# Two MLPs with thirteen Strassen-Winograd units and residual sums in place, and a ReLU bias in the state-space mixer

## The chip, the cores and the metric

The kernel runs on one core of a Trainium2 chip. The metric is the device time of one execution in microseconds (us), lower is better. The core has a matrix engine (TensorE, PE in the profile, with its weight loads as PEld), VectorE (DVE), ScalarE (ACT), GpSimd (POOL) and SyncE (SP), which issues nearly all transfers. Each engine works through its own queue in order and waits on semaphores for the others.

## The reference

A trunk of two layers works on 512 tokens and 16 learned ones ahead of them, 528 columns of 1024 features, in float32. Layer 0 mixes with retention and gated delta-rule heads, layer 1 with a Mamba-2 state-space mixer; each mixer is followed by an MLP with squared ReLU, and each of the four sublayers ends in a layer norm:

```python
h = layer_norm(DN_ALPHA * h + mix, ln1_w[i], ln1_b[i])
h = layer_norm(DN_ALPHA * h + sq_relu_mlp(h, mlp_w1[i], mlp_w2[i]), ln2_w[i], ln2_b[i])

def sq_relu_mlp(h, w1, w2):                      # w1: 1024 x 4096, w2: 4096 x 1024
    return jnp.square(jax.nn.relu(h @ w1)) @ w2
```

In the state-space mixer the attention of a chunk is weighted by `exp(gcum_t - gcum_s)` for s up to t, where `gcum` is the running sum of the log decays of a head.

## The kernel before

**Layout and precision.** Activations lie transposed, features on the 128 partitions in 8 tiles and the tokens along the columns, in two halves of 272 and 256 columns (256 and 256 from the second residual of layer 1 on, where the learned tokens are dropped). Every product of float32 numbers is done as three matmuls of reduced-precision parts (L172 to L174): the activation is kept as a pair `hi`, `lo`, with `hi` the rounded value and `lo` the rest, and each weight tile is fetched and then split on the chip (`split`, L152 on ScalarE and L153 on VectorE). A weight tile of 1024 columns is one such split. `phase` runs over output tiles and evacuates each half from PSUM through a function it is given; in layer 1's MLP a third entry of the activation list holds both halves side by side, so that one matmul covers 512 columns.

**Order.** The program is written as straight code with generators beside it: `spawn` adds one to a list, and `tick` advances each by one step, so that a task's instructions fall between the matmuls of the main line. A planner then places each engine's instructions, near to the order in which they are written, and gives out the buffers. Tiles of a kind (`m`: 24, `s`: 40, `w`: 12 for weights, `row`: 3) share a pool, and PSUM has 3 + 5 banks (`pm`, `px`).

**Layer norm.** `residual` sums `DN_ALPHA * h` and the product of a sublayer in `m` tiles r[half][tile]; `norm_after` transposes these, takes the statistics (L272), normalizes, transposes back (L330) and writes the next activation: `hi` by ScalarE (L337), the full value into a fresh `m` tile t by VectorE (L339), and `lo` as their difference by GpSimd, every fourth by VectorE (L340).

**The MLP.** The 4096 hidden features are 8 groups of 4 tiles. First products of a group (`w1`) give squared ReLUs by ScalarE, GpSimd (L435) and VectorE (L442); second products (`w2`) give a share of the sums over the hidden features for all 8 output tiles, each added to r by `evac0`. The first share finds no r yet: it takes `DN_ALPHA * hi + o` (L366) and then adds `DN_ALPHA * lo` (L367); later shares are one addition (L362). Groups 0 and 1 are done directly, groups 2 to 7 by `Unit`s: a unit does two hidden tiles by Strassen and Winograd's scheme, seven products of half the depth and half the columns (L500, 84 matmuls) in place of eight. It needs combinations of the weights, which `Unit.prepare` makes (L473 to L477 and five splits), and four combinations of the activation for each of 4 pairs of feature tiles, which `combos` makes once for an MLP from the `hi` and `lo` parts (L385 to L401) and splits again. `Four` does the second product of a group for 4 output tiles, with its weights fetched and split ahead. What comes first, up to the first unit's end, is called the head below:

```python
phase([([w1[l, f]], f) for f in range(GF)], hx, ev, ns, head=3, ready=ready)   # group 0
spawn(combos(pairs, nh, get))
for f in range(GF):                                                             # group 1, one tile
    phase([([w1[l, GF + f]], f)], hx, evn, ns)
    if f == 2:
        spawn(stages[0].gen)
    second(0, u, 2 * f, 2 * f + 2)                                              # and two of group 0's second
```

After the head, units and `Four`s alternate: unit (2,0), four (1,0), unit (2,1), four (1,1), up to group 7, whose second product is a `phase` that fetches its weights tile by tile (512 columns) and keeps back the last three output tiles: their half 0 is done for all three, then their half 1 (`tail=3`).

**The mixer's decays.** For each of 4 groups of 8 heads and 4 chunks of 128 columns, `loads` broadcasts `gcum` of the 8 heads over the partitions by a transfer into a `row` tile (128 x 1024). `decays` makes of it `exp(-relu(gcum_s - gcum_t))`: a subtraction on GpSimd (L1181), a ReLU and an exponential on ScalarE (L1182, L1183). GpSimd then multiplies by the chunk's products (L1197), and TensorE takes the result (L1241), together with an operand that VectorE writes (L1202). Beside this the convolutions of the next group of heads run (ScalarE L601 and L604, VectorE L603 and L606).

Of the kernel before, what the change touches and what calls it, by code (L numbers as in the profile page):

```python
# [57 lines left out]
def trunk(ctx: ExitStack, tc: tile.TileContext, a, out):  # L58
# [250 lines left out]
    def norm_after(r, ns, wcol, bcol):  # L309
# [5 lines left out]
        def task(hf):  # L315
# [11 lines left out]
            for m in range(KT):  # L327
# [10 lines left out]
                t = tl("m", n)  # L338
# [33 lines left out]
    def combos(pairs, nh, get):  # L372


        q = slice(0, nh), slice(nh, 2 * nh)

        def part(k, c, lo):
            return pairs[k][lo][:, q[c]].bitcast(F32)

        def diff(out, a, b, engine):  # L380
            engine.tensor_tensor(out, a, b, op=SUB)

        for k in range(4):
            d1, d3, e = tl("m", nh), tl("m", nh), tl("m", nh)
            G.tensor_tensor(d1, part(k, 1, 0), part(k, 0, 0), op=SUB)  # L385
            V.tensor_tensor(e, part(k, 1, 1), part(k, 0, 1), op=SUB)
            V.tensor_tensor(d1, d1, e, op=ADD)
            get(0, k, d1)
            yield
            G.tensor_tensor(d3, part(k + 4, 1, 0), part(k, 1, 0), op=SUB)  # L390
            V.tensor_tensor(e, part(k + 4, 1, 1), part(k, 1, 1), op=SUB)
            V.tensor_tensor(d3, d3, e, op=ADD)
            get(2, k, d3)
            yield
            d2, d4 = tl("m", nh), tl("m", nh)
            G.tensor_tensor(d2, part(k + 4, 1, 0), d1, op=SUB)
            V.tensor_tensor(d2, d2, part(k + 4, 1, 1), op=ADD)
            get(1, k, d2)
            yield
            G.tensor_tensor(d4, part(k + 4, 0, 0), d2, op=SUB)  # L400
            V.tensor_tensor(d4, d4, part(k + 4, 0, 1), op=ADD)  # L401
            get(3, k, d4)
            yield

    def mlp(l, hx, ns, ready, r, evac0, pairs):
# [41 lines left out]

        def second(c, u, m0, m1, tail=0):
            phase([([lambda m=m: wload(second_src(c, m), 512)], m) for m in range(m0, m1)], u,
                  lambda m, hf, o: evac0(m, hf, o, last=c == NG - 1), ns, tail=tail)  # L450
# [110 lines left out]
        u, ev = group()  # L561
        phase([([w1[l, f]], f) for f in range(GF)], hx, ev, ns, head=3, ready=ready)
        spawn(combos(pairs, nh, get))
        stages = []
        un, evn = group()
        groups = [(u, ev), (un, evn)] + [group() for _ in range(2, NG)]
        for c in range(2, NG):
# [947 lines left out]
```

## Time and profile before

| | |
|---|---|
| median of 3 executions | 1738.64 us (1734.0 to 1739.5) |
| the profiled execution | 1738.46 us, span 1736.7 us |
| mean granted TensorE clock | 0.982 |
| transfers | 158.05 MB, 91 GB/s on average |

A row of a group of instructions reads: line, engine, operation, output<-input by the program's names, shape, count, then busy time and the mean of one in ns, then the engine's idle time ahead of them and what ended it. A row in order of time begins with its start and length in us. A wait reads: who waited, for whom, us in total, times, the longest. A stretch reads: its bounds, its length, then the busy time and number of instructions of each engine, the granted TensorE clock, the share of the transfer engines and GB/s. A matmul's row lasts longer than the distance to the next, since they are pipelined; distances are taken from start to start.

### The profile page before, as it was taken

What the parts mean: (1) busy time and instruction counts of PE and PEld (TensorE: products, weight loads), DVE (VectorE), ACT (ScalarE), POOL (GpSimd) and SP (SyncE); (2) the same over time, 40 slices, a digit from 0 to 9 for tenths busy, and PEclk for the clock granted to TensorE, in tenths of its full rate; (3) what the DMA queues carried; (4) which work ended last, traced back from release to release, by engine and by line L of the source; (5) the groups of instructions that cost most, each with busy time, mean ns of one, the idle gap of its engine ahead of it and who ended that gap; (6) DMA issues with size and microseconds to landing.
All of it is one profiled execution on the core that took longest, in us unless ns stands there. A gap on an engine that the chain in (4) does not pass through costs nothing.

```text
span 1736.7 us, 30064 instructions
## 1 busy us (share of the span) xinstructions
PE 1674.2 (96%) x11896; PEld 1542.2 (89%) x11896; DVE 1199.8 (69%) x2383; ACT 700.9 (40%) x1354; POOL 351.1 (20%) x412
## 2 busy tenths in 40 slices
PE   9998999999999899999999998999999998999997
PEld 7897998899999889999998987888778987888886
DVE  5896666766437877767747876767564688777765
ACT  4432235554214344444424643545432434444431
POOL 1211210010003411111102145344410342111112
PEclk9998999999999999999999999999999999999999
DMA  7223212112222232222221443333223123222321
GB/s 243 82 91 86 88 47 84 46 54 84 87 74 68 73 104 98 98 98 98 79 71 62 137 121 92 102 112 98 91 67 110 55 91 110 98 98 98 101 73 69
DMA packets 93002, 158.05 MB, mean 91 GB/s; under 512 B 14077, under 2 KB 47229, under 8 KB 92605
## 3 DMA queue, kind: packets, MB, share of 16 engines
q1 hardware_dynamic: 92716, 155.87, 27.9%
q8 instruction: 93, 1.52, 0.4%
q14 instruction: 49, 0.39, 0.1%
q10 hardware_dynamic: 144, 0.26, 0.0%
HBM read 149.95 MB, written 6.15 MB: 90 GB/s over the span
## 4 chain that ended last, share of the span: by engine, by line
PE 79%; DVE 10%; DMA 4%; POOL 3%; ACT 2%; issue 2%; SPq 0%; POOLq 0%; DVEq 0%; ACTq 0%
PE pmm L172 18%; PE pmm L174 18%; PE pmm L173 18%; PE pmx L500 10%; PE pmm L500 4%; DVE w L153 2%; DVE s L603 2%; DMA row<-rd 1%; DMA w<-in_w 1%; PE pmx L1241 1%; PE pmx L270 1%; DMA du<-row 1%; POOL n L147 1%; PE pmx L1245 1%; ACT w L152 1%
## 5 line engine op out<-in xcount | busy, mean ns | idle before, releaser
L172 PE MATMUL pmm<-hh,w 128*128 128x256 f32 (+5 forms) x1528 | 472.9, 310 | 5.6 <-DVE m L366 2.8
L174 PE MATMUL pmm<-hh,w 128*128 128x256 f32 (+5 forms) x1528 | 459.4, 301 | 2.1 <-DVE w L153 2.1
L173 PE MATMUL pmm<-hl,w 128*128 128x256 f32 (+5 forms) x1528 | 458.4, 300 | 0.7 <-POOL hl L340 0.3
L153 DVE TENSOR_TENSOR w<-w,w 128x1024 fp32r<-128x1024 f32 (+2 forms) x269 | 323.7, 1205 | 142.0 <-PE pmm L173 67.6
L152 ACT CAST w<-w 128x1024 fp32r<-128x1024 f32 (+2 forms) x269 | 263.7, 981 | 373.7 <-PE pmm L174 137.1
L172 PE MATMUL pmm<-s,w 128*128 128x256 f32 (+2 forms) x1180 | 376.8, 319 | 4.3 <-DVE m L366 2.7
L174 PE MATMUL pmm<-s,w 128*128 128x256 f32 (+2 forms) x1180 | 375.5, 318 | 0.2 <-DVE w L153 0.2
L173 PE MATMUL pmm<-s,w 128*128 128x256 f32 (+2 forms) x1180 | 375.5, 318 | 0.0
L172 PEld LDWEIGHTS pmm<-hh,w 128*128 128x128 f32 (+2 forms) x1528 | 289.1, 189 | 20.9 <-issue 4.0
L173 PEld LDWEIGHTS pmm<-hl,w 128*128 128x128 f32 (+2 forms) x1528 | 289.0, 189 | 13.5 <-issue 2.4
L174 PEld LDWEIGHTS pmm<-hh,w 128*128 128x128 f32 (+2 forms) x1528 | 289.0, 189 | 11.4 <-DVE w L153 2.9
L172 PEld LDWEIGHTS pmm<-s,w 128*128 128x128 f32 x1180 | 222.3, 188 | 20.1 <-DVE m L366 3.2
L174 PEld LDWEIGHTS pmm<-s,w 128*128 128x128 f32 x1180 | 222.2, 188 | 15.8 <-DVE w L153 0.6
L173 PEld LDWEIGHTS pmm<-s,w 128*128 128x128 f32 x1180 | 222.2, 188 | 15.2 <-DVE s L1320 0.3
L435 POOL TENSOR_TENSOR m<-m 128x256 f32<-128x256 f32 (+2 forms) x128 | 89.0, 697 | 511.7 <-ACT m L433 499.4
L362 DVE TENSOR_TENSOR m<-m,pmm 128x256 f32<-128x256 f32 (+1 forms) x236 | 93.6, 416 | 71.7 <-PE pmm L174 71.5
L147 POOL TENSOR_TENSOR n<-n,neg 128x1 f32<-128x1 f32 (+2 forms) x58 | 39.8, 690 | 450.4 <-DVE n L146 426.4
L603 DVE SCALAR_TENSOR_TENSOR s<-s,pp,s 128x528 f32<-128x528 f32 x120 | 101.3, 844 | 33.4 <-ACT s L601 31.1
L442 DVE TENSOR_TENSOR s<-m,s 128x256 fp32r<-128x256 f32 (+2 forms) x128 | 69.5, 546 | 51.1 <-POOL m L435 49.9
L500 PE MATMUL pmx<-s,s 128*128 128x264 f32 (+1 forms) x576 | 75.4, 287 | 5.6 <-ACT s L152 5.3
L500 PEld LDWEIGHTS pmx<-s,s 128*128 128x128 f32 x576 | 72.5, 192 | 6.1 <-ACT s L152 5.5
L500 PE MATMUL pmx<-s,w 128*128 128x264 f32 (+1 forms) x576 | 77.6, 284 | 0.0
(312 smaller groups left out, 2368.1 us busy)
## 6 DMA issues: line engine op xcount, KB each, us to landing
w<-in_w SPq DMA_DIRECT2D x88, 512.0 KB, 3.3
w<-in_mw SPq DMA_DIRECT2D x176, 256.0 KB, 3.0
w<-in_mw SPq DMA_DIRECT2D x40, 512.0 KB, 3.2
w<-in_wo SPq DMA_DIRECT2D x29, 512.0 KB, 3.4
row<-rd SPq DMA_DIRECT2D x16, 512.0 KB, 5.7
s<-rd SPq DMA_DIRECT2D x32, 128.0 KB, 5.5
out<-row SPq DMA_DIRECT2D x7, 256.0 KB, 2.0
w<-in_wo SPq DMA_DIRECT2D x6, 256.0 KB, 2.5
```

Source lines behind the costliest of these rows:

```text
L147: G.tensor_tensor(dst, t, neg5[0:part, 0:n], op=POW)
L152: S.copy(dst_hi, src)
L153: V.tensor_tensor(dst_lo, src, dst_hi.bitcast(F32), op=SUB)
L172: T.matmul(o, w[0], x[0], start=first, stop=False)
L173: T.matmul(o, w[0], x[1], start=False, stop=False)
L174: T.matmul(o, w[1], x[0], start=False, stop=last)
L270: T.transpose(pt[m // 4][:bn, (m % 4) * P:(m % 4 + 1) * P], r[m][:, off:off + bn], ident)
L362: V.tensor_tensor(t, t, o, op=ADD)
L435: G.tensor_tensor(q, t, t, op=MUL)
L442: V.tensor_tensor(lo, q, hi.bitcast(F32), op=SUB)
L500: T.matmul(o, w[x][:, c], B[b][k][y], start=first and k == i == 0, stop=last and k == 3 and i == 2, skip_group_check=True)
L603: V.scalar_tensor_tensor(acc, cin[:, k:k + L], w[k], acc, op0=MUL, op1=ADD)
```

## The change

1. `norm_after` writes the normalized value in place, into the sum r that it was made of, so the full float32 activation stays in 16 `m` tiles. The MLP's sums go on in the same tiles (`accumulate`): the first share is one operation on VectorE, `DN_ALPHA * t + o`.
2. `combos` takes its differences from these tiles, all on VectorE. In layer 0, where the halves (272, 256) don't meet the unit's halves of 264 columns, three of the four have a piece of eight columns.
3. Group 1's tiles 1 and 3 become a unit, the first of thirteen. Group 0's second product becomes two `Four`s behind it. The head is now group 0, tiles 0 and 2 of group 1 and that unit.
4. Group 7's second product has its weights prepared by two `Four`s and keeps back four output tiles (`tail=4`).
5. In `decays` GpSimd's subtraction goes; ScalarE does the ReLU for each of the 8 heads by itself, with a column of `gcum` as its bias.

```diff
@@ norm_after
-                t = tl("m", n)
+                t = r[hf][m]
                 V.tensor_scalar(t, pf, w, b, op0=MUL, op1=ADD)
@@
+    def accumulate(h):
+        r, seen = [{}, {}], set()
+        def evac(m, hf, o, last=True):
+            t = h[hf][m]
+            if (m, hf) in seen:
+                V.tensor_tensor(t, t, o, op=ADD)
+            else:
+                V.scalar_tensor_tensor(t, t, DN_ALPHA, o, op0=MUL, op1=ADD)
+                seen.add((m, hf))
...
@@ combos
-            d1, d3, e = tl("m", nh), tl("m", nh), tl("m", nh)
-            G.tensor_tensor(d1, part(k, 1, 0), part(k, 0, 0), op=SUB)
-            V.tensor_tensor(e, part(k, 1, 1), part(k, 0, 1), op=SUB)
-            V.tensor_tensor(d1, d1, e, op=ADD)
-            get(0, k, d1)
-            yield
...
+            q0, q1 = [[quarter(i, c) for c in range(2)] for i in (k, k + 4)]
+            d = [tl("m", nh) for _ in range(4)]
+            diff(d[0], q0[1], q0[0])
+            diff(d[2], q1[1], q0[1])
+            diff(d[1], q1[1], d[0])
+            diff(d[3], q1[0], d[1])
+            for j in range(4):
+                get(j, k, d[j])
+                if j % 2:
+                    yield
@@ mlp
-        for c in range(2, NG):
-            for i in range(2):
-                stages.append(Unit(c, i, lambda f, hf, o, e=groups[c][1]: e(f, hf, o, nh)))
-                stages.append(Four(c - 1, groups[c - 1][0], 4 * i))
-        for f in range(GF):
-            phase([([w1[l, GF + f]], f)], hx, evn, ns)
-            if f == 2:
-                spawn(stages[0].gen)
-            second(0, u, 2 * f, 2 * f + 2)
+        stages = [unit(1, 1), four(0, 0), four(0, 1)]
+        for c in range(2, NG):
+            stages += [unit(c, 0), four(c - 1, 0), unit(c, 1), four(c - 1, 1)]
+        last = [four(NG - 1, 0), four(NG - 1, 1)]
+        gens = [st.gen for st in stages + last]
+        phase([([w1[l, f]], f) for f in range(GF)], hx, groups[0][1], ns, head=3, ready=ready)
+        spawn(combos(h, ns, nh, get))
+        phase([([w1[l, GF]], 0)], hx, groups[1][1], ns)
+        spawn(gens[0])
+        phase([([w1[l, GF + 2]], 2)], hx, groups[1][1], ns)
         until(lambda: "s4" in stages[0].ops and all(x is not None for y in tt for x in y))
...
-        second(NG - 1, groups[-1][0], 0, KT, tail=3)
+        blks = last[0].blks + last[1].blks
+        phase([([[blks[m]]], m) for m in range(KT)], groups[-1][0], evac0, ns, tail=4)
@@ ssd_group, decays
-            G.tensor_tensor(g3(rw, 8), g3(rw, 8), bc(gc[:, c * 32 + 8 * g:c * 32 + 8 * g + 8], P), op=SUB)
-            S.activation(rw, rw, AF.Relu, scale=-1.0)
+            for i in range(8):
+                col = c * 32 + 8 * g + i
+                S.activation(rw[:, i * P:(i + 1) * P], rw[:, i * P:(i + 1) * P], AF.Relu,
+                             bias=gc[:, col:col + 1], scale=-1.0)
             S.activation(rw, rw, AF.Exp, scale=-1.0)
@@ both MLPs
-    r, ev = residual(h, (0, 0), ns0)
+    r, ev = accumulate(r0)
```

More of the change, by code (lines that the diff above doesn't have):

```diff
@@ L405, in mlp, with combos, quarter, diff @@
-    def mlp(l, hx, ns, ready, r, evac0, pairs):
+    def accumulate(h):
[7 more added lines that the diff above has]
+                seen.add((m, hf))
+            if last:
+                r[hf][m] = t
+        return r, evac
+    def combos(h, ns, nh, get):
+        def quarter(k, c):
+            a, b = h[0][k], h[1][k]
+            if c == 0:
+                return [(0, nh, a[:, 0:nh])]
+            cut = ns[0] - nh
+            return ([(0, cut, a[:, nh:ns[0]])] if cut else []) + [(cut, nh, b)]
+        def diff(out, x, y):
+            if not isinstance(y, list):
+                y = [(0, nh, y)]
+            for o, e, ap in x:
+                for o2, e2, ap2 in y:
+                    lo, hi = max(o, o2), min(e, e2)
+                    if lo < hi:
+                        V.tensor_tensor(out[:, lo:hi], ap[:, lo - o:hi - o], ap2[:, lo - o2:hi - o2], op=SUB)
+        for k in range(4):
+            q0, q1 = [[quarter(i, c) for c in range(2)] for i in (k, k + 4)]
[8 more added lines that the diff above has]
+                    yield
@@ L559, in run, with unit, four @@
                             adv()
[L561 to L566, printed above, removed]
-        for c in range(2, NG):
-            for i in range(2):
-                stages.append(Unit(c, i, lambda f, hf, o, e=groups[c][1]: e(f, hf, o, nh)))
-                stages.append(Four(c - 1, groups[c - 1][0], 4 * i))
-        for f in range(GF):
-            phase([([w1[l, GF + f]], f)], hx, evn, ns)
-            if f == 2:
-                spawn(stages[0].gen)
-            second(0, u, 2 * f, 2 * f + 2)
+        groups = [group() for _ in range(NG)]
+        def unit(c, i):
+            return Unit(c, i, lambda f, hf, o: groups[c][1](f, hf, o, nh))
+        def four(c, i):
+            return Four(c, groups[c][0], 4 * i)
+        stages = [unit(1, 1), four(0, 0), four(0, 1)]
+        for c in range(2, NG):
+            stages += [unit(c, 0), four(c - 1, 0), unit(c, 1), four(c - 1, 1)]
[6 more added lines that the diff above has]
+        phase([([w1[l, GF + 2]], 2)], hx, groups[1][1], ns)
         until(lambda: "s4" in stages[0].ops and all(x is not None for y in tt for x in y))
@@ L1365, in trunk @@
     phase([(srcs[m], m) for m in range(3, KT)], yw, ev, ns1, tail=1)
-    h = hn
-    r, ev = residual(h, (0, 0), ns1)
+    h, r0 = hn, r
+    r, ev = accumulate(r0)
     normed = [False, False]
```

43 lines of the change are left out of this document (11 added, 32 removed).

## The prediction

> **What bounds the kernel now.** I read the page's busy times first, then TensorE's own waits over the span and in the first MLP's head, then the stretches where it is idle, then the instructions there in order of time.
>
> ```profile
> PE 1674.2 (96%) x11896; PEld 1542.2 (89%) x11896; DVE 1199.8 (69%) x2383; ACT 700.9 (40%) x1354; POOL 351.1 (20%) x412
> ...
> PE pmx L1241 <- DVE s L1202: 9.6, 4, 4.6
> PE pmm L172 <- DVE m L366: 5.6, 5, 1.5
> PE pmx L500 <- ACT s L152: 5.3, 1, 5.3
> ```
>
> TensorE is busy for 96% of the span, so a change can win in two ways only: fewer matmuls, or shorter waits. The largest waits sit where the change edits: the matmuls of the state-space mixer (L1241) and the head of each MLP (L366 is the first residual sum, L500 the seven products). The stretches show what holds TensorE there (columns: length, then busy time of PE, PEld, DVE, ACT, POOL, then the granted clock):
>
> ```profile
> 557.00:568.50 11.50, 11.50 (x97) 11.50 (x97) 5.12 (x10) 5.21 (x11) 2.73 (x4) 1.00 0.27 90
> 568.50:622.80 54.30, 44.95 (x334) 43.30 (x333) 45.25 (x87) 20.04 (x44) 20.95 (x24) 0.94 0.19 63
> 600.00:616.00 16.00, 9.15 (x59) 8.12 (x58) 15.53 (x28) 5.08 (x10) 4.66 (x6) 0.88 0.19 66
> 1392.30:1449.50 57.20, 51.43 (x231) 42.31 (x230) 51.13 (x101) 22.98 (x49) 23.66 (x26) 0.94 0.29 97
> 1436.00:1444.00 8.00, 2.43 (x16) 1.89 (x15) 6.55 (x14) 2.55 (x6) 3.81 (x5) 0.86 0.38 131
> 1444.00:1448.00 4.00, 4.00 (x18) 4.00 (x19) 4.00 (x9) 2.58 (x5) 0.00 (x0) 0.50 0.00 0
> 916.00:924.00 8.00, 6.28 (x38) 4.44 (x37) 7.41 (x18) 6.16 (x10) 2.52 (x5) 0.93 0.43 145
> 924.00:928.00 4.00, 4.00 (x19) 3.31 (x19) 3.04 (x7) 2.30 (x4) 3.02 (x4) 0.50 0.13 53
> 1465.61:1486.68 21.07, 21.07 (x135) 18.98 (x134) 16.41 (x31) 9.01 (x16) 2.54 (x4) 1.00 0.29 101
> 975.00:1240.00 265.00, 252.16 (x1735) 220.99 (x1734) 189.68 (x280) 129.65 (x219) 112.28 (x83) 0.97 0.39 112
> ```
>
> In the first MLP's head TensorE is idle for 9.4 us and VectorE is full for 15.5 of 16 us around it: VectorE is the bound. In the second head TensorE stands for 5.6 us of 8 and then runs at clock 0.50. At 916 it loses 1.7 us and then 2 us to the clock, between the first MLP and the mixer. The mixer (975 to 1240) loses 12.8 us.
>
> **The change part by part.**
>
> *Thirteen units.* A unit does 84 matmuls where two tiles done directly do 96 of the same width (48 of double width in layer 1). TensorE in order of time; the rows with x12 are the chain's, group 1 begins at 566.87, a unit at 627.57 and 1465.61:
>
> ```profile
> 566.87 0.29 PE L172 MATMUL pmm<-hh,w 128*128 128x272 f32 x1
> 627.57 0.28 PE L500 MATMUL pmm<-hh,w 128*128 128x264 f32 x1
> 637.82 0.29 PE L172 MATMUL pmm<-s,w 128*128 128x272 f32 x1
> 649.74 1.45 PE pmm L500 x12
> ...
> 1454.57 0.40 PE L173 MATMUL pmm<-s,w 128*128 128x512 f32 x1
> 1465.61 1.44 PE pmm L500 x12
> 1475.41 0.40 PE L172 MATMUL pmm<-s,w 128*128 128x512 f32 x1
> 1486.52 0.28 PE L500 MATMUL pmm<-hh,w 128*128 128x256 f32 x1
> ```
>
> Layer 0: a unit takes 637.82 - 627.57 = 10.25 us, the 96 direct matmuls behind it 11.92 (0.124 each): 1.7 us saved. Layer 1: 9.8 against 11.1 (0.2315 each): 1.3 us. But the head is not TensorE's alone, so I work it out as one piece.
>
> *The heads.* VectorE's work in a head now: 24 sums and differences and 16 splits for the combinations, 32 residual operations, the splits of two first-layer and eight second-layer weight tiles beyond those that stay, and the unit's preparation. After: the combinations from the fp32 tiles are 16 wide differences (layer 0: 12 more of eight columns) and 16 splits; the first residual sum is one operation for each half and moves, with the second product of group 0, behind the first unit. There it lies beside full TensorE work and costs nothing as long as VectorE has slack; in a stretch of that kind, 1465.61 to 1486.68, it is busy for 16.4 of 21.1 us. Without that cover, 16 operations of 0.35 would be 6 us for an MLP. What is late next is the unit's own operands, since only 96 matmuls of group 1 are left to hide them. The prices:
>
> ```profile
> 568.54 0.43 DVE L386 TENSOR_TENSOR m<-hl 128x264 f32<-128x264 f32 x1
> ...
> 580.56 1.21 DVE L153 TENSOR_TENSOR w<-w,w 128x1024 fp32r<-128x1024 f32 x1
> 582.04 0.42 DVE L366 SCALAR_TENSOR_TENSOR m<-hh,pmm 128x272 f32<-128x272 f32 x1
> 582.39 0.42 DVE L386 TENSOR_TENSOR m<-hl 128x264 f32<-128x264 f32 x1
> 605.22 0.97 DVE L442 TENSOR_TENSOR s<-m,s 128x256 fp32r<-128x256 f32 x1
> 942.80 0.09 DVE L657 MEMSET m<- 128x32 f32 x1
> ...
> 1392.36 0.42 DVE L442 TENSOR_TENSOR s<-m,s 128x256 fp32r<-128x256 f32 x1 [0.59 <-ACT m L433]
> 1448.74 0.68 DVE L153 TENSOR_TENSOR s<-s,s 128x512 fp32r<-128x512 f32 x1
> ```
>
> Consecutive operations start 0.35 us apart though each lasts 0.42, so 0.07 comes off each row: 0.35 for a wide operation, 0.61 for 512 columns, 1.14 for 1024. An eight-column one is bounded by 0.09 below and 0.35 above; I take 0.10, its size being nearest to the memset's. Layer 0: 32 x 0.35 + 12 x 0.10 = 12.4 for the combinations; the unit's preparation is 4 sums and 3 splits of 512 and 2 splits of 1024, 6.5; one weight split 1.1; four squared-ReLU remainders between 0.35 and 0.90 (605.22, beside GpSimd's square), 2.6 at the middle. That is 22.7 us from 568.54: 591.2. TensorE has 11.9 us of group 1 from 566.87, so it waits from 579. VectorE's own waits in such a head are now 9.05 us of 54.3, some 17%; GpSimd drops out of the combinations and I take 2 us (0 to 3.8). From its last split to the unit's end layer 1 shows 1449.42 to 1454.57, 5.15 us; the second product may start a little later in the new order, so 6.0 (up to 6.8). The unit ends at 599.2. To reach the state that before has at 637.82 there remain group 0's second product, 192 x 0.124 = 23.8, and one unit, 10.25: 633.3. **Layer 0: -4.5 us** (-7.4 with no waits and 5.15, -1.9 with 3.8 and 6.8).
>
> Layer 1 the same way: 32 x 0.34 + 6.5 + 1.1 + six remainders 3.9 = 22.5 from 1392.36, plus 2 and 6.0: 1422.9; plus 96 x 0.2315 = 22.2 and 9.8: 1454.9, against 1454.57. **Layer 1: +0.3 us** (-2.6 to +1.5). Before, its group 1 and second product ran without a stall up to the unit, so taking cover away costs as much as the lighter VectorE work gives.
>
> The half clock is in the 5.15: in 1444 to 1448 the grant is 0.50, and 18 matmuls of 256 columns start where some 33 would, a loss of 1.8 us. The Trainium skill (TensorE: Matmul & The Clock Gate, section What's actually happening) says that an idle window of about 3.4 us halves the clock until a busy window of that length has passed. It speaks against gathering scattered waits into one, as the change does; the 0.50 behind a wait of 5.3 us agrees. By that rule a head would pay 1.7 us on top of the unit's last six products; these are 8.8 us and can start 3.1 us before VectorE's last split ends, so 7.4 would stand in place of my 6.0 and the total would be 1732, as an estimate.
>
> *The mixer's decays.* GpSimd's subtraction goes; ScalarE's one ReLU of 1024 columns becomes eight of 128 with a bias from a tile, sixteen times over.
>
> ```profile
> L1181 POOL TENSOR_TENSOR row<-row,m 128x1024 f32<-128x1024 f32 x16 | 31.7, 1979 | 113.9 <-DMA row<-rd 111.5 <-issue 2.4
> L1182 ACT ACTIVATE row<-row 128x1024 f32<-128x1024 f32 x16 | 17.0, 1061 | 54.9 <-POOL row L1181 53.9 <-POOL s L612 1.0
> 553.49 0.43 ACT L441 ACTIVATE s<-m 128x272 fp32r<-128x272 f32 x1
> 1021.18 0.82 ACT L601 ACTIVATE s<-s,pp 128x528 f32<-128x528 f32 x1
> 1021.90 0.25 ACT L1196 COPY m<-pmx 128x128 f32<-128x128 f32 x1
> 1022.03 2.38 DVE L603 SCALAR_TENSOR_TENSOR s<-s,pp,s 128x528 f32<-128x528 f32 x3 [4.62 <-ACT s L601]
> 1024.44 0.64 ACT L604 ACTIVATE s<-s 128x528 f32<-128x528 f32 x1 [1.34 <-DVE s L603]
> ```
>
> From 272 to 1024 columns ScalarE's time grows 0.84 ns a column, so 128 columns take 0.31; two operands from a tile add 0.18 (0.82 against 0.64), one 0.09. Less the 0.1 by which neighbours overlap (the L601 row of 0.82 is followed after 0.72), a new ReLU costs 0.30; bounds 0.15 (the copy of 128) and 0.40. Eight: 2.4 us against 1.0, so +1.4 us (+0.2 to +2.2) of ScalarE, and -1.98 of GpSimd. ScalarE waited for L1181 53.9 us in all, so mostly the two lie in one line and a chunk's decays end 0.5 us sooner. ScalarE then waits itself for the transfer of the row, for which GpSimd waited 111.5 us. Behind the ReLUs in ScalarE's order wait the convolution's L601, behind it VectorE's L603 and L1202, and for that TensorE (9.6 us in four waits). I count these four at the middle of 0.5 and 1.98 (the larger where another GpSimd operation queues behind the subtraction), -5, and one or two chunks where ScalarE was not waiting for GpSimd at +1.4, the 1.0 of 54.9. **Mixer: -3 us** (-8 with four at 1.98, +4 with none of them and two at 2.2).
>
> *Order at the ends.* With four instead of three tiles kept back, half 0 of the last sums is done 12 x 0.124 = 1.5 us sooner.
>
> ```profile
> 1723.19 0.28 PE L174 MATMUL pmm<-s,w 128*128 128x256 f32 x1
> 1724.79 0.73 DVE L362 TENSOR_TENSOR m<-m,pmm 128x256 f32<-128x256 f32 x2
> ```
>
> At the end VectorE takes the last sums 1.3 us after the last matmul, being busy with half 0's normalization; at 916 half 0 is what TensorE waits for, but half 1 follows at its old time. I take -1 us for each (0 to -1.5, and 0 to -3.7 with the clock). **Ends: -2 us.** The weights of the last product are fetched and split ahead in 1024 columns; TensorE has no wait there now, so nothing. The in-place write of the normalized tile takes the place of a write to a fresh one, at no cost: the transposes that read the old value are long done. SyncE issues the same bytes, group 0's second weights behind the unit's; no wait of TensorE for a transfer shows in these heads.
>
> **The sum:** -4.5 + 0.3 - 3 - 2 = -9.2 us on the profiled execution's 1738.46 (span 1736.7), which stands 0.2 below the median 1738.64: 1729.
>
> **The rivals.**
> (1) *The unit waits as long as the heads waited before.* VectorE takes over GpSimd's differences and the cover shrinks by 33 to 36 us, so layer 0's head ends at its upper bound (-1.9), layer 1's at +1.5, the mixer at 0, the ends at -1: 1737. For it: layer 1's head by my own sum. Against: VectorE's work falls from 45 and 51 us to 23.
> (2) *The differences run early.* They need only the normalized tiles, and VectorE has 6.4 us free of the 11.5 before group 1. If the planner moves them there, each head wins 4 to 5 us more: 1720. Against: L386 needed only such tiles too and ran at 568.54.
> (3) *GpSimd's absence speeds VectorE.* Three L603 took 2.38 us alone; beside two L1181 they took longer:
>
> ```profile
> 979.91 5.62 DVE L603 SCALAR_TENSOR_TENSOR s<-s,pp,s 128x528 f32<-128x528 f32 x3 [0.76 <-ACT s L601]
> ```
>
> That is 1.6 us for each subtraction; if five of sixteen lie on the path, the mixer wins 8, the total is 1724. The Trainium skill (GPSIMD Engine Reference, section 1, Specifications) says GpSimd shares SBUF interfaces with VectorE instructions that have two SBUF inputs, and L603 has two; the row agrees.
> (4) *Slower: ScalarE becomes the mixer's bound.* It is 49% busy there. If a ReLU costs 0.40, a chunk adds 2.2 us; and where ScalarE comes late to the row anyway the 1.98 is not given back. Elsewhere 6.2 us are won, so the total is level when three of the sixteen chunks pass 2.2 us on to TensorE, and slower by more than can be mistaken from six on; eight give 1750, all 1767. Against: 53.9 of the 54.9 us for which ScalarE stood ahead of these ReLUs were waits for L1181.
>
> **How the numbers follow.** My forecast has 0.47, (1) 0.20, (2) 0.10, (3) 0.12, (4) 0.11. About 0.3%, 5.2 us, is what a measurement of this kernel can tell from no change: 1733.4 to 1743.9. The forecast, ranging from 1724 to 1735, falls below that in nine of ten, (2) and (3) wholly, (1) in one of eight: faster 0.67; slower by most of (4) and a little for an order of the planner that I don't foresee, 0.11; the same 0.22. The range 1718 to 1741 leaves out the far ends of (2) and most of (4).
>
> **What the profile after would show.** Right: thirteen units of 84 matmuls in each MLP; no combination on GpSimd; TensorE idle from about 579 for some 7 us, in one run with a half clock behind it; the decays' ReLUs as 128 operations of 0.40 us on ScalarE, busier by some 22 us; GpSimd's 31.7 us of L1181 gone. Wrong: waits at L1241 that grow, or heads in which TensorE stands over 12 us.

## The result, and the profile after

The changed kernel took 1712.53 us (median of four executions, 1711.3 to 1717.2) against 1736.56 for the kernel before: ratio 0.9866, 95% interval 0.9839 to 0.9894. Measured once more beside a variant it took 1717.72 (five executions, 1712.3 to 1718.5) against 1737.13: 0.9881, 0.9862 to 0.9900. So it is faster by 20 to 24 us, where the prediction had 9.2 and a lower end of 1718. The nine executions fall into two groups, 1711.3 to 1713.5 and 1716.8 to 1718.5; what parts one of each is shown at the end of the experiments.

The first page after (span 1709.4, 27.3 us below the span that the prediction worked with), its busy times:

```profile
PE 1661.2 (97%) x11932; PEld 1533.8 (90%) x11932; DVE 1171.2 (69%) x2355; ACT 723.6 (42%) x1458; POOL 295.4 (17%) x364
```

TensorE's largest waits in the changed kernel:

```profile
PE pmx L1020 <- ACT m L1041: 7.0, 1, 7.0
PE pmx L509 <- ACT s L152: 4.3, 2, 3.2
PE pmm L172 <- ACT s L610: 4.1, 2, 3.5
...
PE pmx L1257 <- DVE s L1218: 2.8, 3, 1.3
```

L1257 is the old L1241: its waits for VectorE fell from 9.6 us to 2.8. L509 is the units' products, L610 the copy that ends a convolution's product. ScalarE is busier by 22.7 us, where some 22 were forecast, and GpSimd is busy for 55.7 us less. The groups of instructions that the change made:

```profile
L1197 ACT ACTIVATE row<-row,m 128x128 f32<-128x128 f32 x128 | 41.7, 394 | 31.9 <-DMA row<-rd 31.8
L404 DVE TENSOR_TENSOR m<-m,m 128x256 f32<-128x256 f32 (+2 forms) x40 | 13.4, 371 | 0.0
L381 DVE SCALAR_TENSOR_TENSOR m<-m,pmm 128x256 f32<-128x256 f32 (+1 forms) x32 | 12.8, 416 | 5.1 <-PE pmm L174 5.1
```

The new ReLU is 0.39 us long, and nine in a row took 2.75 us from the first's start to the last's end (kernel with the decays alone), one every 0.29: the price that the prediction took. ScalarE now waits 31.8 us for the transfer of the row, where it waited 53.9 us for GpSimd.

To see where time went, I cut the span of each profile at the same TensorE instructions: the first layer norm's first transpose, the end of unit (2,0) in each MLP, the last unit of layer 0, and the first and last product of a chunk's decays (L1241, after L1257). Lengths in us, worked out from the starts of these matmuls, for the kernels that are told of below:

| kernel | start | head 0 | MLP 0 | into mixer | chunks | head 1 | MLP 1 | end |
|---|---|---|---|---|---|---|---|---|
| before | 478.6 | 159.1 | 241.6 | 129.8 | 258.2 | 187.1 | 231.4 | 50.8 |
| after, first profile | 476.8 | 151.5 | 241.2 | 129.2 | 246.1 | 182.3 | 232.2 | 50.0 |
| after, second | 477.6 | 152.5 | 241.2 | 132.8 | 245.8 | 182.5 | 232.2 | 50.0 |
| decays alone | 480.3 | 159.0 | 241.6 | 128.5 | 245.8 | 187.4 | 231.3 | 51.1 |
| MLPs alone | 479.5 | 151.5 | 241.2 | 127.5 | 258.5 | 182.2 | 231.6 | 49.9 |
| no difference | 479.0 | 159.0 | 241.6 | 129.9 | 250.2 | 187.5 | 231.3 | 50.7 |
| two subtractions added | 478.9 | 151.5 | 241.2 | 129.4 | 252.8 | 182.3 | 232.2 | 50.0 |
| one subtraction added | 479.5 | 151.4 | 241.2 | 129.3 | 250.2 | 181.0 | 232.2 | 50.0 |
| four copies added | 478.6 | 151.4 | 241.2 | 128.7 | 251.1 | 181.0 | 232.2 | 50.0 |
| unit in written order | 478.7 | 154.8 | 241.0 | 129.1 | 246.8 | 190.2 | 232.2 | 50.0 |
| combinations on GpSimd | 478.9 | 155.7 | 241.2 | 130.4 | 245.9 | 184.5 | 232.2 | 50.2 |
| four first | 478.1 | 150.5 | 241.0 | 129.5 | 246.3 | 179.7 | 232.1 | 50.0 |
| twelve units | 478.7 | 146.2 | 241.1 | 131.4 | 246.1 | 179.0 | 231.8 | 49.9 |
| tail of three | 478.4 | 151.6 | 241.2 | 133.1 | 246.0 | 181.0 | 232.2 | 51.0 |
| subtractions in one lump | 478.2 | 151.3 | 241.2 | 148.9 | 246.0 | 182.5 | 232.2 | 50.0 |
| four first, order held | 477.4 | 154.4 | 240.8 | 128.9 | 246.3 | 185.7 | 232.4 | 49.9 |
| unit behind | 477.7 | 151.4 | 241.5 | 133.1 | 246.0 | 182.3 | 231.5 | 50.0 |

Kernels that are the same there repeat within 1.0 us in the chunks (mostly 0.4) and within 1.5 in the heads; the start and the way into the mixer scatter by 3 to 5 us (the 148.9 has a cause, told below). So the gain of 27.3 us is 12.1 in the chunks, 7.6 and 4.8 in the heads, 0.8 at the end, 0.4 and -0.8 in the MLPs' steady parts, and 2.4 in the two scattering pieces. With the new decays eight matmuls, some 1.0 us, stand in the way into the mixer and no longer in the chunks, so 11.1 of the 12.1 are gained there.

### The profile page after: what moved, and what is told of

Its sections match the earlier page's. It is cut to its first block, busy times and chain, and to the rows that moved or that the text cites. A ratio compares the mean times of both kernels' runs of the same rounds, so it can differ in the third digit from the quotient of the medians.

```text
span 1709.4 us, 30161 instructions
## 1 busy us (share of the span) xinstructions
PE 1661.2 (97%) x11932; PEld 1533.8 (90%) x11932; DVE 1171.2 (69%) x2355; ACT 723.6 (42%) x1458; POOL 295.4 (17%) x364
## 4 chain that ended last, share of the span: by engine, by line
PE 85%; DVE 7%; POOL 2%; issue 2%; DMA 2%; ACT 2%; SPq 0%; DVEq 0%; POOLq 0%; ACTq 0%
PE pmm L172 20%; PE pmm L174 19%; PE pmm L173 19%; PE pmx L509 11%; PE pmm L509 4%; DVE s L617 1%; DVE w L153 1%; DMA w<-in_w 1%; PE pmx L270 1%; DMA du<-row 1%; PE pmx L1261 1%; POOL hl L340 1%; PE pmx L1257 1%; POOL n L147 1%; POOL m L448 1%
## 5 line engine op out<-in xcount | busy, mean ns | idle before, releaser
L172 PE MATMUL pmm<-hh,w 128*128 128x256 f32 (+4 forms) x1480 | 454.0, 307 | 6.2 <-ACT s L610 4.1
L173 PE MATMUL pmm<-hl,w 128*128 128x256 f32 (+3 forms) x1480 | 441.6, 299 | 2.4 <-POOL hl L340 1.9
L174 PE MATMUL pmm<-hh,w 128*128 128x256 f32 (+3 forms) x1480 | 442.1, 299 | 0.4 <-DVE w L153 0.4
L152 ACT CAST w<-w 128x1024 fp32r<-128x1024 f32 (+2 forms) x253 | 260.5, 1031 | 367.7 <-PE pmm L174 162.4
L153 DVE TENSOR_TENSOR w<-w,w 128x1024 fp32r<-128x1024 f32 (+2 forms) x253 | 310.7, 1229 | 144.0 <-PE pmm L173 72.0
L172 PE MATMUL pmm<-s,w 128*128 128x256 f32 (+2 forms) x1184 | 377.9, 319 | 0.9 <-ACT w L152 0.5
L174 PE MATMUL pmm<-s,w 128*128 128x256 f32 (+2 forms) x1184 | 376.3, 318 | 0.7 <-DVE w L153 0.7
L172 PEld LDWEIGHTS pmm<-hh,w 128*128 128x128 f32 (+2 forms) x1480 | 277.9, 188 | 20.2 <-ACT s L610 4.6
L173 PEld LDWEIGHTS pmm<-hl,w 128*128 128x128 f32 (+1 forms) x1480 | 278.1, 188 | 14.0 <-POOL hl L340 3.2
L174 PEld LDWEIGHTS pmm<-hh,w 128*128 128x128 f32 (+1 forms) x1480 | 278.1, 188 | 8.8 <-DVE w L153 0.8
L172 PEld LDWEIGHTS pmm<-s,w 128*128 128x128 f32 x1184 | 223.3, 189 | 16.6 <-ACT w L152 0.7
L174 PEld LDWEIGHTS pmm<-s,w 128*128 128x128 f32 x1184 | 223.0, 188 | 16.2 <-DVE w L153 0.9
L617 DVE SCALAR_TENSOR_TENSOR s<-s,pp,s 128x528 f32<-128x528 f32 x120 | 102.3, 852 | 28.2 <-ACT s L615 26.1
L509 PE MATMUL pmx<-s,s 128*128 128x264 f32 (+1 forms) x624 | 81.9, 288 | 5.6 <-ACT s L152 4.3
L446 ACT ACTIVATE m<-row 128x264 f32<-128x264 f32 (+1 forms) x78 | 32.9, 421 | 124.5 <-DVE row L521 114.2
L509 PEld LDWEIGHTS pmx<-s,s 128*128 128x128 f32 x624 | 79.0, 193 | 6.4 <-ACT s L152 4.9
```

Source lines behind the costliest of these rows:

```text
L152: S.copy(dst_hi, src)
L153: V.tensor_tensor(dst_lo, src, dst_hi.bitcast(F32), op=SUB)
L172: T.matmul(o, w[0], x[0], start=first, stop=False)
L173: T.matmul(o, w[0], x[1], start=False, stop=False)
L174: T.matmul(o, w[1], x[0], start=False, stop=last)
L446: S.activation(t, o, AF.Relu)
```

## The experiments

**Each part alone.** The kernel before with the new decays, and the changed kernel with the old ones:

```
 def decays(c, rw):
-    G.tensor_tensor(g3(rw, 8), g3(rw, 8), bc(gc[...], P), op=SUB)
-    S.activation(rw, rw, AF.Relu, scale=-1.0)
+    for i in range(8):  S.activation(..., AF.Relu, bias=gc[:, col:col + 1], scale=-1.0)
```

> The kernel before with the decays' part of the change alone. Theory A (the mixer's gain seen between the two traces, some 9.4 us, belongs to this part): 1736.6 - 9.4, so 1725 to 1729, with the step of 7 to 8 us at the second group of heads. Rival B (my price of 3 us was right, and the rest of the 9.4 is another order that the planner found because the MLP before the mixer changed): 1732 to 1735.

> The changed kernel with the old decays (subtraction on GpSimd, one ReLU of 1024 columns). Theory A (the parts add up): 1712.5 + 9.4, so 1720 to 1724; the heads as in the changed kernel (layer 0 -7.6, layer 1 -4.8 against before). Rival B (the mixer's gain is mostly the planner's new order): 1714 to 1718.

Measured: 1726.44 us against 1736.12 (ratio 0.9942, 0.9929 to 0.9955) and 1722.95 (0.9925, 0.9911 to 0.9939). Theory A: 10.1 and 13.0 us by the ratios, 23 together, what the whole change gives. The chunks take 245.8 us with the new decays whatever the MLPs do, and 258 with the old ones.

**What in the decays gained.** From the products of one chunk to those of the next, the 12.1 us are 3.0 behind the first chunk, 8.1 in three neighbours in the second group of heads (1059 to 1121 us) and 0.9 in one later.

The first place has the path that I had priced. The stretch before and after (length, busy time and number of instructions of PE, PEld, DVE, ACT, POOL, then the granted clock):

```profile
1009.10:1026.60 17.50, 15.32 (x120) 13.81 (x120) 11.95 (x19) 7.16 (x12) 7.45 (x6) 1.00 0.36 106
```

```profile
998.80:1013.20 14.40, 14.30 (x109) 12.79 (x110) 11.81 (x18) 8.76 (x20) 5.75 (x4) 1.00 0.48 129
```

Before, L601 stood behind the subtraction, the ReLU and the exponential and began at 1021.18, 4.8 us after the row's arrival (L1181 began at 1016.42, when the transfer had landed). After, it goes in between the short ReLUs, 1.2 us after the arrival (1006.11 to 1007.27). VectorE's wait for it fell from 4.62 us to 0.90 and TensorE's for the operand behind it from 2.2 to 0.1; the eight matmuls that moved are the other 1.0 us.

The largest place is in the second group of heads. GpSimd and then VectorE of the kernel before in order of time (start, length, instruction, in brackets the idle time ahead and what ended it):

```profile
1065.73 1.90 POOL L1181 TENSOR_TENSOR row<-row,m 128x1024 f32<-128x1024 f32 x1 [5.49 <-DMA row<-rd]
1067.59 3.43 POOL L1289 TENSOR_TENSOR s<-s,s 128x512 f32<-128x512 f32 x2
1070.98 1.89 POOL L1181 TENSOR_TENSOR row<-row,m 128x1024 f32<-128x1024 f32 x1
1072.83 1.04 POOL L1254 TENSOR_TENSOR s<-s,s 128x512 f32<-128x512 f32 x1
...
1090.43 1.90 POOL L1181 TENSOR_TENSOR row<-row,m 128x1024 f32<-128x1024 f32 x1 [4.97 <-DMA row<-rd]
1092.27 0.10 POOL L612 MEMSET s<- 128x3 f32 x1
1092.33 1.04 POOL L1254 TENSOR_TENSOR s<-s,s 128x512 f32<-128x512 f32 x1
```

```profile
1073.91 0.69 DVE L1255 TENSOR_TENSOR s<-s,pmx 128x512 f32<-128x512 f32 x1 [4.04 <-POOL s L1254]
...
1075.94 4.43 DVE L603 SCALAR_TENSOR_TENSOR s<-s,pp,s 128x528 f32<-128x528 f32 x3
...
1093.41 0.69 DVE L1255 TENSOR_TENSOR s<-s,pmx 128x512 f32<-128x512 f32 x1 [3.59 <-POOL s L1254]
```

L1254 scales the mixer's state, L1255 on VectorE adds to it. L1254 is short, but it stands on GpSimd behind L1181, and L1181 stood for a transfer (5.5 and 5.0 us); the first time a second L1181 and two other operations of 3.43 us stand between. VectorE then waited for L1254, with the convolution's L603 and TensorE's operand L1202 queued behind. The same line as a group, before and after (the last two numbers are VectorE's idle time ahead of it, and for whom):

```profile
L1255 DVE TENSOR_TENSOR s<-s,pmx 128x512 f32<-128x512 f32 x12 | 8.2, 679 | 7.6 <-POOL s L1254 7.6
```

```profile
L1271 DVE TENSOR_TENSOR s<-s,pmx 128x512 f32<-128x512 f32 x12 | 8.1, 677 | 0.0
```

All 7.6 us are gone, but not all of them had reached TensorE, and a second chain was as late. ScalarE at the first of the two places:

```profile
1072.90 1.06 ACT L1182 ACTIVATE row<-row 128x1024 f32<-128x1024 f32 x1 [3.09 <-POOL row L1181]
...
1074.12 1.06 ACT L1183 ACTIVATE row<-row 128x1024 f32<-128x1024 f32 x1
1075.08 0.82 ACT L601 ACTIVATE s<-s,pp 128x528 f32<-128x528 f32 x1
```

L601, behind the ReLU that waited for the second L1181, ends at 1075.90, and L603 begins at 1075.94, when VectorE has come free too. So both the queue behind the subtraction and the readers of its result held TensorE there; no run parts the two. The waits had also cost clock. The three stretches, before and after; the same matmuls stand in them:

```profile
1059.00:1082.50 23.50, 18.77 (x162) 17.35 (x161) 17.47 (x28) 9.94 (x17) 12.73 (x9) 0.94 0.35 101
1082.50:1102.90 20.40, 18.35 (x137) 17.26 (x138) 12.55 (x23) 11.81 (x23) 10.29 (x11) 0.90 0.31 91
1102.90:1121.40 18.50, 18.49 (x132) 16.61 (x132) 13.91 (x21) 9.79 (x15) 7.33 (x7) 0.91 0.30 86
```

```profile
1045.70:1065.50 19.80, 18.52 (x162) 17.36 (x162) 16.93 (x26) 11.44 (x27) 7.74 (x5) 1.00 0.41 120
1065.50:1083.10 17.60, 16.93 (x137) 15.44 (x137) 13.41 (x23) 14.11 (x33) 9.01 (x10) 1.00 0.36 105
1083.10:1100.00 16.90, 16.90 (x133) 15.43 (x132) 14.09 (x21) 11.31 (x22) 5.78 (x6) 1.00 0.29 95
```

The third stretch before has no wait at all and is still 1.6 us longer: only the clock. PE's busy times differ by 0.25, 1.42 and 1.59, 3.3 us for the three. Together they are 8.1 us shorter, so the other 4.8 are idle time of TensorE.

**The subtraction left out.** The kernel before without L1181 and with its one ReLU of 1024 columns; the difference of the running sums is left out of the computation.

> The kernel before without the subtraction of the decays' running sums (left out of the computation), with one ReLU of 1024 columns as before: no GpSimd operation and none of the 22 us that the 128 short ReLUs add to ScalarE. Theory S0 (the short ReLUs cost nothing, the gain is the missing subtraction): the same as the kernel with the decays alone within 1.5 us, 1725 to 1729. Rival S1 (the short ReLUs cost up to 1.4 us in chunks where ScalarE is late): 3 to 6 us faster than that kernel. Rival S2 (short ReLUs help, since the planner puts other ScalarE work between them): 2 to 5 us slower than that kernel.

Measured: 1726.09 us (0.9934, 0.9918 to 0.9951; executions from 1721.2 to 1731.0). By the medians S0: taking GpSimd's operation away is worth as much as the whole edit of the decays, so 128 short ReLUs cost nothing that shows. The subtraction is the cause of the gain. L1255 waits 0.0 us for GpSimd here too. The profiled execution, the slowest of six, has chunks of 250.2 us, 4.4 more than with short ReLUs; 1.0 of them are the eight matmuls, which did not move here, 1.1 a stretch at clock 0.91, and in one place VectorE waits 1.4 us for L601, which stands behind two ReLUs and exponentials, where in the kernel with short ReLUs it went in among the second row's ReLUs. Behind the first chunk it shows as well: L601 starts 2.5 us after the row's arrival here (1017.05 to 1019.56), between the 4.8 and the 1.2. Whether that interleaving is worth something over many executions stays open, since the medians are alike.

**GpSimd's load put back, with nobody waiting.** Two subtractions of 128x512 for each chunk, first on a scratch tile of their own:

```
+    for _ in range(2):  G.tensor_tensor(g3(scr, 8), g3(scr, 8), bc(gc[...], 64), op=SUB)
     for i in range(8):  S.activation(..., AF.Relu, ...)
```

> The changed kernel, with two subtractions of 128x512 on GpSimd put back for each chunk, on a scratch tile of their own: nothing waits for their values, ScalarE's ReLUs do not. GpSimd is loaded as before, about 2 us a chunk. Theory G (what counted was GpSimd's time: operations queued behind it and VectorE operations slowed beside it): 6 to 9 us of the gain go, 1718 to 1722. Rival H (what counted was that ScalarE's ReLU stood behind the subtraction, and the convolution behind the ReLU): 1711 to 1715.

Measured: 1733.48 us (0.9987, 0.9977 to 0.9997), worse than both theories, for a reason of its own. As nothing held them, all 32 ran in one lump ahead of the chunks. GpSimd and ScalarE there:

```profile
954.20 17.80 POOL L1198 TENSOR_TENSOR scr<-scr,m 128x512 f32<-128x512 f32 x13 [22.71 <-DVE m L1157]
971.94 0.10 POOL L626 MEMSET s<- 128x3 f32 x1
```

```profile
972.08 0.83 ACT L615 ACTIVATE s<-s,pp 128x528 f32<-128x528 f32 x1 [8.84 <-POOL s L626]
```

A memset of 0.10 us for the next convolution stood behind 17.8 us of them, ScalarE waited for it, and TensorE for ScalarE: 19.9 us of waits for L610. It does not tell G from H, but it shows at another place what a short operation costs that stands in GpSimd's order behind long ones. In the chunks themselves, free of the lump, the time was 246.0, as in the changed kernel.

So they were tied to the chunk, by reading the tile gx that is fetched with the row; then half of them; then copies in their place:

```
+    for _ in range(2):  G.tensor_tensor(g3(scr, 8), g3(gx, 8), bc(gc[...], 64), op=SUB)   # then range(1)
+    for _ in range(4):  G.tensor_copy(scr, gx)                                              # in their place
```

> The changed kernel with two subtractions of 128x512 on GpSimd for each chunk, as in the run before, but they now read the tile gx that is fetched together with the chunk's row, so that they cannot run ahead: GpSimd gets its 2 us a chunk where the old subtraction stood, and no one waits for the values. Theory G (GpSimd's time counted: operations queued behind it, VectorE operations slowed beside it): 6 to 9 us of the mixer's gain go, 1718 to 1722. Rival H (that ScalarE's ReLU and the convolution behind it stood behind the subtraction): 1711 to 1715.

> The changed kernel with one subtraction of 128x512 on GpSimd for each chunk that reads gx, half of what cost 7.9 us. Theory G (GpSimd's time costs by the amount): half of that, 1715.5 to 1717.5. Rival K (it costs only where GpSimd's work passes what a chunk has room for): 1711.5 to 1714.

> The changed kernel with four copies of gx (128x512) on GpSimd for each chunk in place of the two subtractions that cost 7.9 us; nobody waits for them. Theory R (VectorE's operations with two inputs are slowed by GpSimd's subtractions, which also read two): copies slow VectorE less, VectorE's busy time stays within 5 us of the changed kernel's 1171, and the loss is under 4 us. Rival Q (GpSimd's later operations queue behind): the loss goes with GpSimd's added busy time at about 0.19 us for each us, whatever the operation is, with VectorE's operations unslowed.

Measured: 1720.44 us (0.9902, 0.9886 to 0.9918), 1716.97 (0.9888, 0.9869 to 0.9907) and 1717.39 (0.9885, 0.9868 to 0.9901). Against the changed kernel's 1712 to 1718 only the first stands out; the chunks, which repeat within 1.0 us, tell more: 252.8, 250.2 and 251.1 against 246, so 6.8, 4.2 and 5.1 us lost. The pages' busy times, in this order:

```profile
PE 1662.8 (97%) x11932; PEld 1534.5 (89%) x11932; DVE 1185.1 (69%) x2355; ACT 723.9 (42%) x1458; POOL 336.1 (20%) x396
```

```profile
PE 1662.7 (97%) x11932; PEld 1534.8 (90%) x11932; DVE 1180.2 (69%) x2355; ACT 723.4 (42%) x1458; POOL 316.2 (18%) x380
```

```profile
PE 1662.9 (97%) x11932; PEld 1534.8 (90%) x11932; DVE 1182.8 (69%) x2355; ACT 724.0 (42%) x1458; POOL 348.4 (20%) x428
```

GpSimd is busier by 41, 21 and 53 us than after's 295.4, VectorE by 13.9, 9.0 and 11.6 than 1171.2, with the same 2355 instructions. The first two lie in theory G's ranges. The loss does not follow GpSimd's time (copies: most time, middle loss), so Q falls in that form. It goes with VectorE's: 0.49, 0.47 and 0.44 us lost for each us that VectorE's operations grew. R's numbers for copies fall as well (11.6, not under 5; 5.1, not under 4): copies slow VectorE too. Which of VectorE's operations are slowed shows in two groups, after and with two subtractions added:

```profile
L617 DVE SCALAR_TENSOR_TENSOR s<-s,pp,s 128x528 f32<-128x528 f32 x120 | 102.3, 852 | 28.2 <-ACT s L615 26.1
```

```profile
L617 DVE SCALAR_TENSOR_TENSOR s<-s,pp,s 128x528 f32<-128x528 f32 x120 | 110.0, 917 | 28.8 <-ACT s L615 26.5
L1274 DVE TENSOR_TENSOR s<-s,pmx 128x512 f32<-128x512 f32 x12 | 8.1, 679 | 1.6 <-POOL s L1273 1.6
```

L617, with two inputs from SBUF, the on-chip memory, grows from 852 ns to 917 (904 with one subtraction, 900 with copies). L1274, the old L1255, takes one input from PSUM and stays as it was (677 ns after, 679 here). So work on GpSimd beside VectorE slows VectorE: rival 3 of the prediction, a true effect. The Trainium skill (GPSIMD Engine Reference, section 1, Specifications) says that GpSimd shares its SBUF interfaces with VectorE, with contention where a VectorE instruction has two SBUF inputs; the rows agree. That this slowing makes up the whole loss is not shown, since some queueing stands beside it: VectorE waits 1.6 us for GpSimd at L1274 with two subtractions and 2.1 with copies, where it waited for none. For L1181 itself contention is small: VectorE's busy time fell from 1199.8 to 1192.1 with the decays alone, and 7.7 at 0.47 is an estimated 3.6 us, part of it hidden in the waits above. L603, by which rival 3 had priced it, did not gain at all (120 of them 101.3 us before, 102.1 with the decays alone).

**The heads: what fills the unit's wait.** TensorE of the changed kernel in layer 0, from the first unit on:

```profile
578.59 0.28 PE L509 MATMUL pmm<-hh,w 128*128 128x264 f32 x1
579.40 0.39 PE L172 MATMUL pmm<-s,w 128*128 128x272 f32 x1 [0.54 <-ACT w L152]
...
585.31 0.51 PE L509 MATMUL pmx<-s,s 128*128 128x264 f32 x2 [3.23 <-ACT s L152]
586.51 0.59 PE L174 MATMUL pmm<-s,w 128*128 128x272 f32 x1 [0.69 <-DVE w L153]
...
587.81 3.66 PE L509 MATMUL pmx<-s,s 128*128 128x264 f32 x22
591.31 3.10 PE L509 MATMUL pmx<-s,w 128*128 128x264 f32 x24
...
595.72 0.28 PE L173 MATMUL pmm<-s,w 128*128 128x272 f32 x1
```

The unit is not one wait and seven products. The rows of L172 and L174 that read s are group 0's second product: the planner put 9 of its matmuls between the unit's in layer 0, and 24 in layer 1 (1382.00 to 1389.02), 1.1 and 5.6 us of work that my sum placed behind the unit. To test it, TensorE was held to the written order:

```
+    if i == 0: fixed.enter_context(tc.manual_schedule(engines={PE}))   # closed after i == 1
     st.run(adv)
```

> The changed kernel with TensorE held to the written order through the first unit and the second product behind it. Theory F (what my heads missed is that the planner puts matmuls of the second product into the unit's waits: 9 of 0.124 us in layer 0 and 24 of 0.2315 us in layer 1 stand there, 1.1 and 5.6 us): 5 to 7 us slower, 1717 to 1720. Rival E (the heads gain because VectorE is done earlier than I took it to be): 1711 to 1714.

Measured: 1724.68 us (0.9927, 0.9913 to 0.9942), 7 to 12 slower; heads of 154.8 and 190.2 against 151.5 and 182.3, 3.3 and 7.9 more. That is theory F and some 2.2 us on top in each. Most of this is a further product: the planner also did a second of the unit's own seven, 12 matmuls, ahead of the wait (580.35 to 581.80 in layer 0), and in the written order it stands behind (595.45 on). So 9 + 12 and 24 + 12 matmuls moved, 2.6 and 7.0 us, and TensorE's idle time from the unit's start to its end grew by as much (4.7 to 7.4 us, and 2.3 to 9.3). The rest, 0.7 and 0.9, is left for the clock. Layer 0's head after, and in written order:

```profile
579.00:593.00 14.00, 9.47 (x59) 8.86 (x60) 11.92 (x32) 7.40 (x16) 0.21 (x1) 0.88 0.23 75
```

```profile
580.00:594.00 14.00, 6.57 (x31) 6.06 (x30) 12.20 (x32) 7.12 (x16) 0.72 (x1) 0.64 0.18 54
```

With the matmuls in between, the longest idle time is 3.23 us and the mean grant 0.88; without them it is 6.4 us and 0.64, and the unit ends 8.0 us after VectorE's last split (591.86 to 599.86), with 57 of its matmuls left behind that split, in place of 5.6 (590.08 to 595.72) with 46. The prediction took 6.0. It had 7.4 by the rule of the Trainium skill (TensorE: Matmul & The Clock Gate, What's actually happening) that an idle window halves the clock; behind the gathered wait the grant is 0.50 from 584 to 594 us, so the trace agrees, and the 8.0 is nearer to the rule's value.

**The differences back on GpSimd**, from the same fp32 tiles (one letter in `diff`: `V.tensor_tensor` to `G.tensor_tensor`).

> The changed kernel with the combinations' differences on GpSimd instead of VectorE. Theory V (in the heads VectorE's amount of work sets the unit's end): VectorE loses some 6 us a head and the unit ends up to 6 us earlier, 1703 to 1710. Rival C (the differences are a chain into VectorE's splits, longer on GpSimd, and VectorE's operations with two inputs run slower beside them): 1716 to 1726.

Measured: 1721.79 us (0.9915, 0.9900 to 0.9930): in rival C's range. Head 0 is 155.7 (+4.2) and head 1 184.5 (+2.2), though VectorE lost some 6 us of work in each (13.4 us of L404 in both); TensorE's waits for L152 in the units grew from 4.3 to 7.7 us. The differences are the first link of a chain into ScalarE's copy and VectorE's remainder, and GpSimd is the slower place for it (40 of them take 29.8 us there).

**Other places for the first unit.** Behind one half of group 0's second product; the same with TensorE in written order; behind both halves; and no thirteenth unit, with group 1 all direct:

```
-stages = [unit(1, 1), four(0, 0), four(0, 1)]
+stages = [four(0, 0), unit(1, 1), four(0, 1)]    # four first, and with the order held
+stages = [four(0, 0), four(0, 1), unit(1, 1)]    # unit behind
+stages = [four(0, 0), four(0, 1)]                # twelve units; group 1 all direct ahead
```

> The changed kernel with the first unit placed behind the first half of group 0's second product (four output tiles) instead of ahead of both halves. Theory V (in the head TensorE waits for VectorE's combinations, 7.1 us in layer 0 and 4.5 us in layer 1, and the second product that could cover it stands behind): most of the 11.6 us comes back, 1701 to 1706. Rival P (the planner had already pulled forward what can be, and the sums of the second product now stand ahead of the splits on VectorE): 1709 to 1714.

> The kernel with the first unit between the halves of group 0's second product, now with TensorE held to the written order through these two stages. Theory O (that kernel gained only 3 us because the planner put the unit's products ahead of 48 matmuls of the second product, and TensorE waited 4.5 us and ran at half clock with this work behind it): 1701 to 1705. Rival W (the written order is the worse one, as for the unit held to it): 1709 to 1714.

> The changed kernel with the first unit placed behind both halves of group 0's second product, so that it keeps the thirteenth unit and has 24 us of cover more. Theory V (only the uncovered place of the unit costs): the time of the kernel with twelve units less the unit's savings of 1.7 and 1.3 us, 1700 to 1702. Rival D (now two units stand next to each other, and VectorE with some 9.7 us of work for a unit of 10.1 us falls behind): 1703 to 1707.

> The changed kernel with the thirteenth unit undone: group 1 all direct (192 matmuls ahead as cover), then group 0's second product, no unit in the head; the sums in place stay. Theory V: the unit's saving (1.7 and 1.3 us) goes and the wait (7.1 and 4.5 us) with it, 1702 to 1706. Rival P (the wait only moves: the second product's sums in place must wait for the combinations to be read): 1710 to 1716.

Measured: four first 1709.31 us (0.9837, 0.9820 to 0.9854); order held 1717.29 (0.9879, 0.9861 to 0.9897); unit behind 1714.92 (0.9867, 0.9848 to 0.9887); twelve units 1703.71 (0.9808, 0.9791 to 0.9825). Theory V holds for twelve units alone; four first lies in rival P's range, and the other two are slower than either of their theories said. TensorE's waits between 560 and 640 us, in the kernel with the order held and then with the unit behind:

```profile
PE pmm L172 <- DVE m L381: 6.0, 2, 5.0
```

```profile
PE pmm L172 <- DVE m L381: 4.6, 1, 4.6
```

In these two the unit no longer waits, but the second product does: each of its results is added in place on VectorE (L381), behind the combinations and splits, and TensorE stands until a result is taken. It is no cover, since it needs the engine that is late. Group 1's direct products are one, needing nothing of these. The stretch from group 1's start over both products and a unit, in the kernel with twelve units:

```profile
565.00:625.00 60.00, 59.92 (x491) 59.70 (x490) 43.28 (x96) 27.39 (x56) 11.62 (x12) 1.00 0.26 88
```

TensorE does not stop in it. Head 0 is 5.3 us shorter than after and head 1 3.3, though a unit's saving (1.7 and 1.3) is given up in each. This version beats both kernels: 33 us below the kernel before (30 to 36), and 10 to 13 below the changed one by the ratios.

**The ends, and the measure itself.** Three tiles kept back instead of four; and the changed kernel again.

> The changed kernel with three instead of four tiles kept back in the last second product of both MLPs. Theory T (the 2.9 us that the way into the mixer gained and the 0.8 us at the end belong to the fourth tile): 1715 to 1717. Rival N (they came of another order around it, or of chance): 1711 to 1714.

> The changed kernel once more, as the measure for its variants. If the first profile's start, in which the first unit begins 1.5 to 2.7 us earlier than in the profiles of six variants with the same code up to there, was chance: 1712 to 1715, the first unit at 578.5 to 580. If it was not: 1711 to 1712 and the unit again at 577.

Measured: 1716.68 us (0.9882, 0.9865 to 0.9899) and 1717.72 (0.9881). The first lies in theory T's range, but the changed kernel itself, measured once more, is not faster, so the medians tell nothing of the fourth tile. The last piece is 51.0 us with three tiles and 50.0 with four: 1.0 us at the end is the tile's. The way into the mixer is 133.1 with three, but the changed kernel itself, with four, has 129.2 in one profile and 132.8 in the other, so theory T falls there. The same stretch of the changed kernel in its two profiles:

```profile
909.60:919.60 10.00, 9.29 (x69) 7.78 (x70) 9.29 (x19) 6.72 (x12) 4.60 (x6) 1.00 0.17 54
```

```profile
911.30:921.30 10.00, 9.29 (x47) 7.30 (x48) 7.88 (x15) 6.45 (x11) 4.61 (x6) 0.66 0.16 54
```

Same program, same 9.29 us busy, 69 matmuls at grant 1.00 or 47 at 0.66: some 3 us, by nothing that the program sets. It is more than half of the 5.2 us between these two profiles; whether it also parts the other executions isn't shown. The Trainium skill (TensorE: Matmul & The Clock Gate, What's actually happening) says that the window by which the clock is set runs freely, so that the number of slow matmuls at a kernel's start varies from run to run; this pair shows a variation of that kind in the middle of a kernel, and that the window is its cause is not shown. My guess of 1712 to 1715 for the second measurement missed; the first unit began at 577.96 there, between the two values, so the early start was chance at most in part.

## Why the prediction was wrong

- **Mixer, -3 us: the term that failed most; the chunks gave -12.1.** The failing step is "I count these four at the middle of 0.5 and 1.98": -5 for the four waits at L1241, and +2 for chunks where ScalarE is late. The waits were the right ones and fell by 6.8 us (9.6 to 2.8): in order of time 2.2 became 0.1, 4.6 became 1.3 and 2.0 none, each by more than the 1.98 that the step allowed, while the fourth did not fall. At the first it was the priced chain alone, shortened further as L601 went in between the short ReLUs. At the next two L1254, and behind it VectorE, stood in GpSimd's order behind the subtraction and its wait for a transfer, beside the priced chain. The lower clock behind the waits, 3.3 us, was in no term, though the prediction had priced it in the heads, and the +2 did not come. Another 1.0 is the eight matmuls that moved. The ReLU's price and ScalarE's 22 us held, and hid.
- **Rival 3** (-8 from five slowed places) came nearest in the mixer, but contention is an estimated 3.6 us, and not where it was priced; its rival, the queue, shows in L1255's row. **Rival 4** shows at one place, the 3.5 us wait for L610, which takes the place of another wait there (3.7 us in the kernel with the MLPs alone), and is no loss on the whole.
- **Head of layer 0, -4.5; measured -7.6.** "There remain group 0's second product, 192 x 0.124" failed by 9 matmuls, 1.1 us, done inside the unit's waits. Most of the rest is that the unit ended 1.7 us sooner than the forecast 599.2 (595.72, and the head began 1.76 us earlier): VectorE was done 1.4 us sooner. In the order that the step assumed the head is 154.8 - 159.1 = -4.3, near the forecast by luck: VectorE sooner by 1.5, and the unit's end 8.0 us behind its last split for the 6.0 taken. The one wait of some 7 us that I looked for came in pieces, the longest 3.23.
- **Head of layer 1, +0.3; measured -4.8.** The same step failed by 24 matmuls of 0.2315, 5.6 us for a miss of 5.1; the unit itself ended as forecast (1400.56, and the chunks had ended 22.46 us earlier, so 1423.0 for 1422.9). In the assumed order it is 190.2 - 187.3, the mean of the three heads as before, +2.9, outside the stated -2.6 to +1.5: there too the unit's end lay further behind the last split than the 6.0 (8.9 us, 1399.66 to 1408.56).
- **Ends, -2.** At the end -0.8 for -1. Into the mixer nothing shows above a scatter of 4 us.
- **Rival 1** (as long a wait as before, 1737) falls. **Rival 2** half came: not the combinations but the unit's weight sums moved ahead of group 1 in layer 0 (560 to 563.7 us). Its 1720 is the nearest total, for another reason than its own. **Rival 4's** point of decision, three chunks with 2.2 us passed on, was not reached.
- Missed: the steady part of the second MLP is 0.8 us longer. A slip without effect: the middle of 0.35 and 0.90 is 0.63, so the squared-ReLU remainders are 2.5 and 3.8 us, not 2.6 and 3.9.

## What to carry to other kernels

Price a removed instruction by what stands behind it on its in-order engine and whom that keeps waiting, including its own wait for a transfer, not only by its length and by who reads its result. When work is moved to cover a wait, ask whether the cover itself needs the engine that is late: here only products that need nothing of VectorE's combinations were cover, and giving up one cheaper unit for them won 10 to 13 us. Before a stage is summed, ask which later work that needs nothing of it can be done inside its waits: here that was up to 7.0 us. A price for idle time needs its clock term everywhere, and differences of 3 us need the segments of several profiles, not two medians.

## What was not expected of the hardware

- One short instruction on GpSimd behind long ones kept ScalarE idle for 8.84 us (the memset of 0.10 us behind 17.8 us of subtractions).
- Plain copies on GpSimd slow VectorE's operations too: 64 copies of 128x512 with no second input made 2355 VectorE instructions 11.6 us longer in all.
- One 10 us stretch of the same program ran at a mean grant of 1.00 in one execution (69 matmuls) and of 0.66 in another (47), with the same busy time and no wait of TensorE longer than 0.95 us in it.
